# When additions of weights are issued in attention, and which of two ready pieces of work goes first at the start of the MLP

## The chip, the core and the metric

The kernel runs on one core of a Trainium2 chip. The metric is the time of one execution in device microseconds (us). Five engines work side by side, each through its own list of instructions in a fixed order: TensorE (PE) multiplies and transposes, VectorE (DVE) and ScalarE (ACT) do elementwise work, GpSimd (POOL) does some elementwise work and issues the DMAs that add to HBM, and SyncE (SP) issues the other DMAs. An engine whose next instruction waits runs nothing that stands behind it.

## The reference

One decoder layer on x of 512 tokens by 1024 channels, in float32:

```python
h = rms_norm(x, norm_mix)
u, q, kc, vc, ksl, vsl, kwn, vwn, g_nsa, g_merge = split(h @ w_in)
y_pool = pool_mixer(u, w_pool, pool_scale)
y_nsa  = nsa_mixer(q, kc, vc, ksl, vsl, kwn, vwn, g_nsa, ...)   # 16 heads
g_a, g_b = split(sigmoid(g_merge))
x = x + (g_a * (y_pool @ w_proj_pool) + g_b * (y_nsa @ w_proj_nsa)) @ w_out
h = rms_norm(x, norm_mlp)
x = x + square(relu(h @ w_ff1)) @ w_ff2
return rms_norm(x, norm_final)
```

The attention has a compressed, a selected and a window branch. With 512 tokens, all eight blocks of keys are selected.

## The kernel before

**Precision.** A float32 operand of a large product is split into a high part (a copy in a reduced form, by ACT) and a low part (the rest, by DVE). A product is the sum of high times high, high times low and low times high.

**Strassen-like products.** The gates, `w_out` and the MLP use seven products of quarters where eight would be plain: `A11, S3, S1, S2, A12, A22, S4`. The names beginning with S need sums of quarters of the weights. The kernel makes these sums in HBM: a *job* is first a copy of one quarter into a scratch tensor, issued by SP (`make_sum`, line 340), and then an accumulating DMA that adds the other quarter to it, issued by POOL (`add_sum`, line 348). There are 55 jobs, numbered 0 to 54 in the order of their copies. Copied jobs whose addition has not been emitted stand in the queue `begun`, the oldest first.

**Loads.** All weights pass through 170 loads of 512 KB or less, numbered 0 to 169, into six buffers named `raw`. `emit_load` (line 299) issues the next load and behind it the copies that are due at it (`sums_after`). A load leaves the table `raws` when both of its parts have been converted. Loads 37 to 49 are the weights of the gate and of the queries that fill up PE in attention (`FILL2`), 50 to 57 those of `w_proj_nsa`, 58 to 71 those of `w_out`, 72 and later those of the MLP. By `sums_after`, job 16 is copied behind load 47, jobs 17 and 18 behind 48, 19 behind 49, 20 and 21 behind 50, and one each (22 to 25) behind loads 51 to 54. Jobs 17, 20 and 25 copy a sum that is itself a job (9, 12 and 21), so `make_sum` first emits all additions up to that job. From load 54 on, `emit_load` emits one addition at each load while more than two jobs are in `begun`.

**Attention.** Scores are worked off in 96 slots, twelve for each of eight pairs of heads. In slot i PE forms the scores of i+1 and turns the probabilities of slot i-4 (line 1440), DVE masks and takes the maximum of i (line 1400), ACT takes the exponential (line 1410), and POOL multiplies the probabilities of slot i-1 by the reciprocal of their sum and by the gate (`weight`, line 1423). Every third slot after the seventh, when no rotation of queries is under way (`scored["rope"]`), an addition may be emitted behind that multiplication (`add_sum(last)`). Such an addition is tied to its slot by `tc.issue_after`; additions that `make_sum` and `emit_load` emit have no such tie.

**Order.** The kernel is written as one sequence with generators that interleave; a planner then fixes each engine's order ahead of time. It takes what it expects to be ready, by priority, which is the place in the program unless `high_priority` raises it. `behind(ins)` puts what follows on the engine of `ins` after it in that order, without a wait of its own.

**The start of the MLP.** `Mixed` multiplies the merged mixers by `w_out`. Its `take` adds the products to x (line 1706 for `S1` and `A22`), sums the squares, scales the tokens (`scaled`: a reciprocal, line 1602, and two multiplications, line 1612) and turns them on PE in `to_fm` (line 1864). Tokens come in four tiles of 128: tiles 0 and 1 after `A22`, tiles 2 and 3 after `S4` (line 565). `S4` accumulates in the two PSUM tiles of `S1`, so it waits until line 1706 has read them. The scaled tiles go through the turning into high and low parts (line 1868 and 1871). Then come the MLP's first products on PE (line 635), for two groups 0 and 1, called in the order `A11100, A11101, A12100, A12101`: the product's name, the layer, the chunk, the group. `A12100` accumulates on `A11100`'s PSUM tile, after ACT has copied that tile (line 650). All PSUM tiles here carry one tag with eight buffers, and the program asks for them in the order: `A11100`, two for turning token tile 2, `A11101`, two for tile 3.

Of the kernel before, what the change touches and what calls it, by code (L numbers as in the profile page):

```python
# [62 lines left out]
def trunk(ctx: ExitStack, tc: tile.TileContext, A, out):  # L63
    nc = tc.nc
    PE, ACT, DVE, POOL = nc.tensor, nc.scalar, nc.vector, nc.gpsimd
# [104 lines left out]
    for k in P1 + FILL2:  # L170
        if k[-2] == "G":
            g, o = int(k[-1]), k[:-2]
# [15 lines left out]
    late, later, wo_of = [], [], []  # L188
# [80 lines left out]
    raws, hls = {}, {}  # L269
    st = {"load": 0, "prep": 0, "use": 0, "kept": 0, "pairs": 0, "sums": 0, "spared": 0}  # L270
    spare, slots_hl = [], []
    held, begun = {}, deque()

    began, conv = [None], [None]

# [57 lines left out]
    def make_sum(load):  # L333

        if st["sums"] < len(jobs):
            to, q, _ = jobs[st["sums"]]
            while any(q is jobs[n][0] for n in begun):
                add_sum()
            with tc.issue_after(load.ins):
                nc.sync.dma_start(to, q)  # L340
            begun.append(st["sums"])
            st["sums"] += 1

    def add_sum(behind=None):

        to, _, q = jobs[begun.popleft()]
        with tc.issue_after(behind.ins) if behind else nullcontext():
            POOL.dma_start(to, q, accum_op=ALU.add)  # L348

    part, first_of, held_back, roots, summed = {}, [], [], [], []  # L350
# [231 lines left out]
    def step_side():  # L582
        for _ in range(len(side)):
            g = side.popleft()
            try:
                next(g)
                side.append(g)
            except StopIteration:
                pass
# [9 lines left out]
    def product(ps, key, first, mm):  # L599

        w, n = use(key), 0
        for f in range(2):
            for low in range(2):
                for k, u, v in [(k, low, v) for k in range(4) for v in range(2 - low)]:
                    mm(ps[:, 256 * f:256 * f + 256], w, f, k, u, v, start=first and n == 0, stop=n == 23,
                       skip_group_check=True)
                    n += 1
                    if n % 6 == 0:
                        step_side()
                        ahead()  # L610

    def until(ready):
        while not ready():
            assert side
            step_side()

    class Group:


# [6 lines left out]
        def pe(self, o):  # L626
            until(lambda: o not in self.NEEDS or self.NEEDS[o] in self.done)
            if not self.done:
                side.append(self.main())
            name, x, *at = self.X[o]  # L630
            until(lambda: self.of(x))
            moving = self.of(x)

            def mm(out, w, f, k, u, v, **kw):
                PE.matmul(out, w[u][:, k, 128 * f:128 * f + 128], moving[v][:, k, :], **kw)  # L635
            if not at:
                self.ps[name] = self.bank()
            product(self.ps[name], o + self.key, not at, mm)
            if at:
                side.append(self.last(name, *at))  # L640
            self.done.add(o)
# [30 lines left out]

    hT = (R1, R2)
    f_banks = [2]
    last_mm = [None]

    def fm_products(wH, wL, xT, sub=0, nk=8, tok=slice(0, S)):
        prods = []
# [104 lines left out]
    def behind(made):  # L783
        return tc.issue_after(made.ins)
# [41 lines left out]
    r, _ = evac0(1)  # L826
    with behind(r):
        r, scaled2 = sums0(2)
# [4 lines left out]
    with behind(conv[0]):  # L833
        root3, v = sums0(3)
# [34 lines left out]
    scored = {"pairs": 0, "rope": 0}  # L869
# [70 lines left out]
    with ExitStack() as c1:  # L940
# [254 lines left out]
        for k in P1[2:]:  # L1195
            i = int(k[-1]) if k[-1].isdigit() else None
            if k[-2] == "G":
                if not gate_f:
                    t = p1.tile([128, 16, 128], FR, tag="cA", bufs=1, name="gs")
# [29 lines left out]
            elif k[:2] == "pp":  # L1229
                w = use(k)  # L1230
# [17 lines left out]
    with ExitStack() as c2:  # L1248
# [200 lines left out]
        def turn_hi(i):  # L1449
            src, dH, dL = turn_views(i)  # L1450
            his.append(ACT.activation(dH, src, AF.Copy))  # L1451
# [46 lines left out]
        for i in range(n + LAG + PLAG):  # L1498
            if i < n:
                p = slots[i][0]  # L1500
                if i % 12 == 3 and p + 1 < NPAIR:
                    while p + 1 not in Q:
                        fill()
                        step_side()
                if i % 12 == CMP_AT and p + 1 < NPAIR:
                    side.append(cmp_scores(p + 1))
            if i + 1 < n:
                score_pe(i + 1)
                scored["pairs"] = (i + 2) // 12
            t = i - LAG  # L1510
            if 0 <= t < n:
                turn_pe(t)
                turn_hi(t)
            if i < n:
                smax(i)
                expo(i)
            if 0 <= i - 1 < n:
                last = weight(i - 1)
                slot.update(long=i > 3 and slots[i - 1][1] == 1, scaled=last)
            if i > 7 and i % 3 == 0 and not scored["rope"] and len(begun) > 2:  # L1520
                add_sum(last)
            if 0 <= t < n:
                slot["low"] = turn_lo(t)
            step_side()
            want = done0 + (total - done0) * (i + 1) // (n + LAG + PLAG)
            while fdone[0] < want and fill():
                pass
            if i < 5:
                fill()
            if turning:  # L1530
                turn_c()
            j = t - PLAG
            if 0 <= j < n and j % 2 == 1 and pv(j):
                o_evac(*slots[j][0:2])
# [185 lines left out]
    with ExitStack() as c3:  # L1720
# [7 lines left out]
        for m, keys in enumerate(("A112o0 A122o1 S42o0", "A112o1 A222o0 S42o1", "S32o0 A222o1 A11100", "S32o1 S12o0 A11101")):  # L1728
            for k in keys.split():
                o = 1024 * m + 8 * (k[:2] in ("S1", "S3", "A2"))  # L1730
# [70 lines left out]
        class Mixed(Wide):  # L1801
# [25 lines left out]
            def take(self, o, ps):  # L1827
                yield from super().take(o, ps)
                if o == "S2":
                    for i, j in ((1, 0), (1, 1), (0, 1)):  # L1830
                        for f in range(2):
                            x = XX[:, 2 * j + f, 512 * i:512 * i + 512]
                            DVE.tensor_tensor(x, x, self.U[:, f, :], op=ALU.subtract if i else ALU.add)
                            yield
                elif o == "A12":
                    for t in range(2):
                        square_sum(t, 0)
                elif o == "S1":
                    for t in range(2, 4):
                        square_sum(t, 1, 0)  # L1840
                elif o == "A22":
                    for t in range(2):
                        square_sum(t, 1)
                    xs = [scaled(t) for t in range(2)]
                    while "S1" not in self.done:
                        yield
                    for t in range(2):
                        yield from to_fm(t, xs[t])

        def scaled(t):  # L1850
            xs = q3.tile([128, D], F32, tag="xs", bufs=2, name="xs")
            normed(t, xs)
            return xs

        def to_fm(t, xs=None):
            if xs is None:
                xs = scaled(t)
                for _ in range(3):
                    yield
            th, sl = t // 2, slice(128 * (t % 2), 128 * (t % 2) + 128)  # L1860
            for a in range(2):
                pt = bank()
                for k in range(4):
                    PE.transpose(pt[:, 128 * k:128 * k + 128], xs[:, 512 * a + 128 * k:512 * a + 128 * k + 128], ident)
                src = pt[:, :].rearrange("p (k c) -> p k c", k=4)
                b = f"{a + 1}{th + 1}"
                if b != "12":
                    ACT.activation(XB[b][0][:, :, sl], src, AF.Copy)
                ACT.activation(XQ[b][:, :, sl], src, AF.Copy)
                if b != "12":  # L1870
                    DVE.tensor_tensor(XB[b][1][:, :, sl], src, XB[b][0][:, :, sl].bitcast(F32), op=ALU.subtract)
                yield
            shaped.append(t)
            if th == 0:
                return
            for o, d, x, y in (("T1", XT, XQ["11"], XQ["12"]), ("T3", XQ["12"], XQ["22"], XQ["12"]),
                               ("T2", XQ["11"], XQ["22"], XT)):
                DVE.tensor_tensor(d[:, :, sl], x[:, :, sl], y[:, :, sl], op=ALU.add if o == "T2" else ALU.subtract)
                while o not in XB:
                    yield  # L1880
                ACT.activation(XB[o][0][:, :, sl], d[:, :, sl], AF.Copy)
                yield
                DVE.tensor_tensor(XB[o][1][:, :, sl], d[:, :, sl], XB[o][0][:, :, sl].bitcast(F32), op=ALU.subtract)
            turned[0] += t == 3
# [206 lines left out]
    t, o = 3, out_of(3)  # L2091
# [3 lines left out]
    with tc.high_priority(64):  # L2095
        ACT.activation(junk[0], ps, AF.Square, accum_out=sq[:, t, 1:2])
        r = rms(t)
# [22 lines left out]
```

## Time and profile before

| | |
|---|---|
| median of three runs | 766.87 us (766.41 to 767.01) |
| the profiled execution | 766.66 us |
| its span, first to last instruction | 764.9 us |
| around the span | 1.8 us |
| mean granted TensorE clock | 0.997 of 2.4 GHz |
| stretch of the attention's slots | about 172 to 362 us |
| start of the MLP | about 437 to 453 us |

Times inside the profile count from the start of the span. In a timeline row stand the start, the busy time, the engine, the line, the operation, the shapes and how many instructions were merged; in brackets the idle time of that engine just before, and what ended it by the profile.

### The profile page before, as it was taken

The page shows a single profiled execution, that of the slowest core. Times are in us where ns is not written, and L with a number is a line of the kernel's source. Part 1 is how long each engine was busy: PE and PEld are TensorE (multiplying, and loading weights), DVE is VectorE, ACT ScalarE, POOL GpSimd, SP SyncE. Part 2 cuts the span into 40 slices and gives each one's busy share as a digit, 9 for nine tenths or more (in the row PEclk, how much of TensorE's full clock was granted, in tenths as well). Part 3 has the DMA queues.
Part 4 walks back from the last instruction along what each step waited for, and adds up shares of the span by engine and source line. Part 5 has one row for each costly group of instructions (what it writes and reads, how often), then busy time and mean ns, then how long its engine had stood idle before and what let it go on. Part 6 is the DMA issues. An engine that isn't in the chain of part 4 may idle for free.

```text
span 764.9 us, 13254 instructions
## 1 busy us (share of the span) xinstructions
PE 752.9 (98%) x4661; PEld 669.7 (88%) x4661; DVE 670.8 (88%) x1282; ACT 513.2 (67%) x977; POOL 190.5 (25%) x269
## 2 busy tenths in 40 slices
PE   8999999999999999999999999999999999999996
PEld 7889999888888888888888799989998999899985
DVE  7998989549989889989689999998899788978897
ACT  7777655328878888898746576944774477447754
POOL 5001010117747876875000020111111111110001
PEclk9999999999999999999999999999999999999998
DMA  9869886986063945675383699979999999798532
GB/s 303 227 177 275 230 245 143 250 215 165 18 204 83 224 94 115 121 139 111 89 296 133 218 272 249 298 210 325 290 269 211 315 307 263 206 313 252 195 109 110
DMA packets 120285, 158.09 MB, mean 207 GB/s; under 512 B 6006, under 2 KB 88474, under 8 KB 119963
## 3 DMA queue, kind: packets, MB, share of 16 engines
q1 hardware_dynamic: 98058, 127.62, 51.2%
q0 software_dynamic: 21872, 28.84, 24.4%
q10 hardware_dynamic: 288, 0.79, 0.3%
q8 instruction: 37, 0.61, 0.3%
q14 instruction: 30, 0.24, 0.1%
HBM read 152.50 MB, written 59.77 MB: 278 GB/s over the span
## 4 chain that ended last, share of the span: by engine, by line
PE 87%; DVE 6%; ACT 2%; DMA 2%; issue 1%; POOL 1%; ACTq 0%; DVEq 0%; POOLq 0%; SPq 0%
PE psB L1685 21%; PE psB L635 21%; PE psF L565 18%; PE psV L635 5%; PE psB L565 4%; PE psS L1378 4%; PE psO L1474 3%; PE psT L1440 3%; PE psV L565 2%; PE psF L697 2%; DMA S<-w_ff 1%; PE psC L997 1%; DVE P L1400 1%; DVE PT L1456 1%; PE psT L565 1%
## 5 line engine op out<-in xcount | busy, mean ns | idle before, releaser
L348 POOL DMA_DIRECT2D S<-w_ff x44 | 49.3, 1124 | 334.1 <-DMA S<-w_ff 247.9
L395 ACT ACTIVATE wh<-raw 128x1024 fp32r<-128x1024 f32 x72 | 76.1, 1058 | 75.6 <-PE psB L635 28.3
L565 PE MATMUL psF<-R,wh 128*128 128x512 f32 x384 | 124.5, 400 | 0.0
L1423 POOL TENSOR_SCALAR P<-P,sm,GT 128x128 f32<-128x128 f32 (+3 forms) x128 | 91.0, 798 | 45.5 <-DVE sm L1420 25.4
L401 DVE TENSOR_TENSOR wl<-raw,wh 128x1024 fp32r<-128x1024 f32 x72 | 87.9, 1221 | 10.2 <-ACT wh L395 9.7
L565 PEld LDWEIGHTS psF<-R,wh 128*128 128x128 f32 x384 | 68.8, 188 | 11.2
L1410 ACT ACTIVATE P<-P,sm 128x128 f32<-128x128 f32 (+3 forms) x128 | 71.0, 557 | 9.6 <-DVE sm L1400 6.3
L565 PE MATMUL psF<-R,wl 128*128 128x512 f32 x192 | 75.5, 393 | 0.0
L521 ACT ACTIVATE wh<-raw 128x512 fp32r<-128x512 f32 (+1 forms) x76 | 45.1, 616 | 31.0 <-PE psF L565 21.2
L1400 DVE CUSTOM_DVE_ANT_0 P<-psS,cst 128x128 f32<-128x128 f32 (+3 forms) x128 | 59.5, 483 | 5.2 <-PE psT L1440 3.7
L395 ACT ACTIVATE w3h<-raw 128x1024 fp32r<-128x1024 f32 x36 | 38.1, 1058 | 36.9 <-PE psB L635 15.4
L524 DVE TENSOR_TENSOR wl<-raw,wh 128x512 fp32r<-128x512 f32 (+1 forms) x74 | 50.9, 697 | 11.0 <-ACT wh L521 10.2
L1451 ACT ACTIVATE PT<-psT 128x512 fp32r<-128x512 f32 (+2 forms) x96 | 49.0, 520 | 13.8 <-PE psT L1440 12.8
L1456 DVE TENSOR_TENSOR PT<-psT,PT 128x512 fp32r<-128x512 f32 (+2 forms) x96 | 56.2, 592 | 1.2 <-ACT PT L1451 1.0
L1440 PE MATMUL psT<-ident,P 128*128 128x128 f32 x320 | 50.2, 273 | 0.3 <-POOL P L1423 0.3
L401 DVE TENSOR_TENSOR w3l<-raw,w3h 128x1024 fp32r<-128x1024 f32 x36 | 44.0, 1222 | 5.6 <-ACT w3h L395 5.4
L1474 PE MATMUL psO<-PT,VV 128*128 128x256 f32 x320 | 48.5, 286 | 0.0
L635 PE MATMUL psB<-R,wh 128*128 128x256 f32 x336 | 46.7, 279 | 0.7 <-ACT GB L650 0.7
L1440 PEld LDWEIGHTS psT<-ident,P 128*128 128x128 f32 x320 | 39.5, 140 | 8.8 <-POOL P L1423 0.8
L635 PEld LDWEIGHTS psB<-R,wh 128*128 128x128 f32 x336 | 42.6, 188 | 1.1 <-ACT GB L650 0.9
L1474 PEld LDWEIGHTS psO<-PT,VV 128*128 128x128 f32 x320 | 42.2, 188 | 1.3 <-ACT PT L1451 0.3
L565 PEld LDWEIGHTS psF<-R,wl 128*128 128x128 f32 x192 | 36.0, 188 | 7.5
(450 smaller groups left out, 2074.6 us busy)
## 6 DMA issues: line engine op xcount, KB each, us to landing
raw<-w_ff SPq DMA_DIRECT2D x54, 512.0 KB, 6.0
S<-w_ff POOLq DMA_DIRECT2D x44, 512.0 KB, 8.5
raw<-S SPq DMA_DIRECT2D x44, 512.0 KB, 5.6
S<-w_ff SPq DMA_DIRECT2D x32, 512.0 KB, 7.6
raw<-w_in SPq DMA_DIRECT2D x31, 512.0 KB, 5.4
S<-S SPq DMA_DIRECT2D x12, 512.0 KB, 5.8
S_o<-w_out POOLq DMA_DIRECT2D x8, 512.0 KB, 7.8
raw<-w_proj_nsa SPq DMA_DIRECT2D x8, 512.0 KB, 4.5
```

The lines of the kernel that those rows point to most:

```text
L395: ACT.activation(h, t, AF.Copy)
L401: DVE.tensor_tensor(l, t, h.bitcast(F32), op=ALU.subtract)
L524: eng.tensor_tensor(l[:, sl], t[:, sl], h[:, sl].bitcast(F32), op=ALU.subtract)
L565: PE.matmul(ps, a, b, start=first and j == 0, stop=last and j == n - 1, skip_group_check=True)
L635: PE.matmul(out, w[u][:, k, 128 * f:128 * f + 128], moving[v][:, k, :], **kw)
L1400: DVE.tensor_tensor_reduce(out=P[:, o:o + n].rearrange("p (a c) -> p a c", c=128), in0=s, in1=m, scale=1.0, scalar=3e38, op0=ALU.add, op1= ...
L1410: last_exp[:] = [ACT.activation(c, c, AF.Exp, bias=sm[:, 0, e:e + 1], scale=-1.0, accum_out=sm[:, 1, e:e + 1])]
L1423: r = POOL.tensor_scalar(P[:, o:o + n], P[:, o:o + n], sm[:, 2, e:e + 1], GT[:, qb, c + e:c + e + 1], op0=ALU.mult, op1=ALU.mult)
L1440: PE.transpose(pt[:, 128 * j:128 * j + 128], P[:, 128 * j:128 * j + 128], ident)
L1456: return DVE.tensor_tensor(dL, src, dH.bitcast(F32), op=ALU.subtract)
L1474: PE.matmul(ps[:, qb % 2, :, :], VV[:, k, b, g, :], t[:, j, :, :], start=False, stop=last and j == len(kbs) - 1 and t is tL, skip_group_ch ...
L1685: PE.matmul(ps[f], self.Y.of(y)[u][:, 2 * g + k, 128 * f:128 * f + 128], w[v][:, k, :], start=first and g == k == u == v == 0, stop=g == k ...
```

## The change

Three edits. In the attention, an addition is emitted when at least two jobs are in `begun` and every load up to the second one after the oldest job's copy has been converted, where before it was emitted when more than two jobs were in `begun`. The first multiplication of `A12100` is put behind the last of the latest `A11` product, which is `A11101`'s. Token tile 1's scaling is emitted after `S1` has been taken and put behind `S1`'s additions to x on DVE.

```diff
+    held, begun, born = {}, deque(), {}
...
             begun.append(st["sums"])
+            born[st["sums"]] = st["load"] - 1
             st["sums"] += 1
+
+    def landed():
+
+        return len(begun) > 1 and min(raws, default=st["load"]) > born[begun[0]] + 2
...
-            if i > 7 and i % 3 == 0 and not scored["rope"] and len(begun) > 2:
+            if i > 7 and i % 3 == 0 and not scored["rope"] and landed():
                 add_sum(last)
...
             def mm(out, w, f, k, u, v, **kw):
-                PE.matmul(out, w[u][:, k, 128 * f:128 * f + 128], moving[v][:, k, :], **kw)
+                late = o + self.key == "A12100" and f == k == u == v == 0
+                with behind(last_mm[0]) if late else nullcontext():
+                    r = PE.matmul(out, w[u][:, k, 128 * f:128 * f + 128], moving[v][:, k, :], **kw)
+                if o == "A11":
+                    last_mm[0] = r
...
-                    xs = [scaled(t) for t in range(2)]
+                    xs = scaled(0)
                     while "S1" not in self.done:
                         yield
-                    for t in range(2):
-                        yield from to_fm(t, xs[t])
+                    with behind(summed[0]):
+                        other = scaled(1)
+                    yield from to_fm(0, xs)
+                    yield from to_fm(1, other)
```

(`last_mm = [None]` moves up to stand before the class that now uses it.)

## Rows read from the trace of the kernel before

**Rows 1.** The page: busy time and share of each engine.

```profile
PE 752.9 (98%) x4661; PEld 669.7 (88%) x4661; DVE 670.8 (88%) x1282; ACT 513.2 (67%) x977; POOL 190.5 (25%) x269
```

**Rows 2.** Busy time by stretch: length, PE, PEld, DVE, ACT, POOL, clock, DMA.

```profile
172.00:362.00 190.00, 188.35 (x1220) 165.75 (x1219) 172.64 (x578) 161.96 (x443) 130.45 (x193) 1.00 0.58 126
...
438.00:453.00 15.00, 13.70 (x93) 12.20 (x92) 14.46 (x25) 11.06 (x26) 5.36 (x5) 1.00 1.04 305
453.00:742.00 289.00, 289.00 (x1908) 265.28 (x1907) 261.21 (x312) 182.11 (x243) 26.42 (x24) 1.00 0.92 257
```

**Rows 3.** What PE waited for, attention's slots, then 380 us to the end.

```profile
PE psS L1378 <- DVE sm L1400: 1.1, 3, 0.5
PE psT L1440 <- POOL P L1423: 0.3, 1, 0.3
PE psO L1465 <- ACT PT L1451: 0.3, 1, 0.3
...
PE psB L635 <- ACT GB L650: 0.7, 1, 0.7
PE psB L565 <- DVE x L1706: 0.6, 1, 0.6
```

**Rows 4.** The chain of waits between 255 and 280 us: start, us, what.

```profile
260.24 10.00 DMA S<-w_ff
```

**Rows 5.** Timeline of POOL in attention.

```profile
230.65 1.10 POOL L348 DMA_DIRECT2D S<-w_ff  x1 [1.21 <-DMA S<-w_ff]
...
244.96 1.07 POOL L348 DMA_DIRECT2D S_o<-w_out  x1
...
253.23 2.06 POOL L348 DMA_DIRECT2D S_o<-w_out  x1
256.53 1.17 POOL L348 DMA_DIRECT2D S<-w_ff  x1 [1.24 <-DVE sm L1420]
...
270.87 1.19 POOL L348 DMA_DIRECT2D S<-w_ff  x1 [4.98 <-DVE PT L1456]
```

**Rows 6.** Timeline of SP in attention: issues of copies.

```profile
220.01 0.59 SPq L340 DMA_DIRECT2D S<-w_ff  x1
...
224.93 0.59 SPq L340 DMA_DIRECT2D S<-w_ff  x1
...
244.91 0.54 SPq L340 DMA_DIRECT2D S<-S  x1
...
275.16 0.59 SPq L340 DMA_DIRECT2D S<-w_ff  x1
```

**Rows 7.** Attention's additions (line 348): from issue to landing.

```profile
DMA to landing us min/median/max: 6.1/6.4/11.5
```

**Rows 8.** Timeline of PE at the start of the MLP.

```profile
437.04 1.14 PE L1864 MATMUL psB<-ident,xs 128*128 128x128 f32 x9
438.80 0.47 PE L565 MATMUL psB<-W1H,mH 128*128 128x512 f32 x1 [0.61 <-DVE x L1706]
...
445.19 1.10 PE L635 MATMUL psB<-R,W1H 128*128 128x256 f32 x8
...
448.86 0.51 PE L635 MATMUL psB<-R,wh 128*128 128x256 f32 x2 [0.69 <-ACT GB L650]
...
449.88 0.60 PE L1864 MATMUL psB<-ident,xs 128*128 128x128 f32 x4
450.23 0.95 PE L635 MATMUL psB<-R,W1H 128*128 128x256 f32 x6
```

**Rows 9.** Timeline of DVE in the same stretch.

```profile
435.12 1.42 DVE L1612 SCALAR_TENSOR_TENSOR xs<-x,sq,gB 128x512 f32<-128x512 f32 x2
...
437.97 1.28 DVE L1706 TENSOR_TENSOR x<-x,psB 128x512 f32<-128x512 f32 x2
439.17 1.22 DVE L401 TENSOR_TENSOR W1L<-raw,W1H 128x1024 fp32r<-128x1024 f32 x1
...
447.61 1.41 DVE L1612 SCALAR_TENSOR_TENSOR xs<-x,sq,gB 128x512 f32<-128x512 f32 x2
```

More of the change, by code (lines that the diff above doesn't have):

```diff
@@ L271, in trunk @@
     spare, slots_hl = [], []
-    held, begun = {}, deque()
+    held, begun, born = {}, deque(), {}
     began, conv = [None], [None]
@@ L615, in until @@
             step_side()
+    last_mm = [None]
     class Group:
@@ L674, in trunk @@
     f_banks = [2]
-    last_mm = [None]
     def fm_products(wH, wL, xT, sub=0, nk=8, tok=slice(0, S)):
```

## The prediction

> **What bounds the kernel now.** I read the page first. PE is busy 98% of the span [rows 1], so only two things can shorten the kernel: less work on PE, or less idle time of PE. The change removes no multiplication and no transposition, so all of its gain or loss must be PE's idle time. Busy time by stretch shows where that idle time is [rows 2]. From 453 to 742 us there is none: 289.00 us busy of 289.00. In attention's slots PE lacks 1.65 us of 190, and at the start of the MLP 1.30 us of 15. Both are places that the change touches. What PE waited for names the pieces [rows 3]: in attention three waits on DVE's maxima (1.1 us in all), one on ACT (0.3) and one on POOL (0.3); at the start of the MLP one on ACT's copy of `A11100`'s tile (0.7) and one on `S1`'s additions by DVE (0.6). These sum to 3.0 us. That is the ceiling of what the change can win.
>
> After 453 us PE never waits, so what PE gains or loses before then reaches the end, unless a later stage has it waiting for something else. DMA's share there is 0.92 [rows 2], so there is little room for transfers that are pushed into it.
>
> The chain of waits shows what the attention's edit is about [rows 4]: a copy for a sum, issued at 260.24, took 10.00 us, and POOL's addition stood waiting for it. The timeline of POOL says the same, with a name that misleads [rows 5]: the addition at 270.87 was preceded by 4.98 us of idle time, put down to a DVE instruction; but the copy landed at 260.24 + 10.00 = 270.24, and the addition followed 0.63 us behind. The multiplications of the probabilities stood behind it, and PE lost 0.3 us to them [rows 3].
>
> **Which additions the new test moves.** I followed the two conditions through the program's own counters, slot by slot. Before, of the 17 additions emitted in the slots (jobs 7 to 23), ten are tied to a slot (7, 10, 11, 13 to 18, 23), and seven (8, 9, 12, 19 to 22) are emitted without a tie, because a copy needs an earlier sum or because load 54 is reached. The timeline shows what a missing tie does [rows 5]: jobs come in order of number in the program, yet job 19's addition, at 230.65, stands ahead of job 7's, at 244.96, the first of the two into `w_out`. The planner puts an untied addition where it expects the copy to have landed: 19's copy was issued at 224.93 [rows 6].
>
> With the new test, jobs 7 and 10 stay in slots 36 and 39. Job 11 (the one at 253.23) fails in slot 42, since load 45 is not converted, and is then emitted untied when load 50 needs job 12. Job 13 goes from slot 60 to 75, and 14, 15 and 16 move on by three slots each, to 78, 81 and 84. Jobs 17, 18 and 23 lose their ties: 17 and 18 are emitted when load 54 needs job 21, job 23 when load 55 is reached. Job 22, the one that stalled POOL at 270.87, is untied before and after. So the edit does not make that addition wait for its copy in the program; it changes the company the copy travels in. Nothing is issued later than the last tied addition of before, and copies and loads keep their order.
>
> **The price in attention, part by part.** *Job 11 leaves 253.23.* It probably goes ahead of the slots, before 172 us, where POOL has nothing to multiply. Between 244.96 and 270.24, 25.3 us, five additions (the first at 244.96, the last at 256.53) and three copies for sums (the first at 244.91 [rows 6], the last at 260.24) ran beside a few loads: at most an estimated 25.3 / 8 = 3.2 us each. One fewer lands job 22's copy up to 3.2 us earlier, and POOL's 4.98 us wait falls to as little as 1.8. Since the whole wait cost PE 0.3 us [rows 3], the bounds are 0 and -0.3. I take -0.3: what is left of the stall is likely to be covered by the slots that lie between POOL's multiplication and PE's turning.
>
> *Jobs 17 and 18 come early.* Their copies are issued one behind the other, the second at 220.01 [rows 6]. Uncrowded, a copy lands in about 5.1 us (job 19's: 230.65 less the 0.63 us between landing and issue, less 224.93). So these additions are probably issued at about 225 and 226, while job 19's copy, issued at 224.93, is under way. At 3.2 us each they delay it by up to 6.4 us, and job 19's wait of 1.21 us grows to as much as 7.6. The nearest row for such a wait is the 4.98 us one, which cost 0.3 us; beyond that I count one for one. Bounds: 0 and 0.3 + 2.6 = +2.9. I take +0.1: the three overlap only in part, and a wait near 4 us is below the row's.
>
> Here the profile and a page differ. An addition alone took at least 6.1 us from issue to landing, at the median 6.4 [rows 7]. The Trainium skill, DMA: Bandwidth & Descriptors, section Anatomy of one DMA, gives a fit of 2.0 us plus the bytes over 436 GB/s, 3.2 us for 512 KB. By it POOL would hardly wait for either copy, and both terms would be nothing.
>
> *Job 23 is untied.* Its copy, at 275.16 [rows 6], has no addition beside it but job 22's. The addition comes at about 281 instead of at the attention's end; a wait of up to 2 us lies inside what the 4.98 us wait shows to be nearly free. 0. *Jobs 13 to 16* have landed long before; each addition takes POOL about 1.1 us wherever it stands [rows 5], and POOL is busy for 130 of 190 us [rows 2]. 0. Should the cover go, each costs its 1.1 us.
>
> **The price at the start of the MLP.** *Token tile 1's scaling.* DVE scales tile 0 at 435.12 for 1.42 us, then tile 1, and only at 437.97 takes `S1` [rows 9]. PE had issued `S1` by 437.04 and waits 0.61 us for that until 438.80 [rows 8]. After the change `S1` is taken at about 436.8 and `S4` can begin at about 438.0, when the eight transpositions of tile 0 are through. This saves PE 0.6 to 0.8 us at that point. But DVE runs on without a pause afterwards, 14.46 of 15 us [rows 2], and the same instructions remain. A gap of about 0.25 us arises between 436.54 and 436.8, as nothing else may go there: the low parts of the next weights are themselves behind `S1`. So tile 2's scaling, at 447.61 [rows 9], comes about 0.25 us later.
>
> *`A12100` behind `A11101`.* `A11101` has the same tokens as `A11100`, which starts at 445.19, and its weights' low part is made from 439.17 on [rows 9]. Yet `A12100` went first, at 448.86 with 0.69 us of waiting, and `A11101` followed only at 450.23, right behind the turning of token tile 2 [rows 8]. The one thing left that can hold it is its PSUM tile, which the program asks for after the two of tile 2. I take it that tiles of a tag are given out in the program's order. Then PE has nothing to run between `A11100` and tile 2's turning after the change: the wait on ACT goes, and a wait on tile 2 takes its place. Scaling of tile 2 ends at 449.02 + 0.25; its last four transpositions follow at 449.33 and end, at the 0.35 us of before, at 449.68. The four multiplications of `A12100` that ran before this point, and now do not, cost half of the 1.10 us that eight take at 445.19, 0.55 us. Equal work is done at 450.23, as before. I take 0 for both edits together. Bounds: -1.3 if both waits go for good, and +1.2 if one of DVE's conversions of 1.22 us [rows 9] comes ahead of a scaling.
>
> **Sum.** -0.3 + 0.1 + 0 = -0.2 us on the profiled execution: 766.66 - 0.2 = 766.46, a span of 764.7 and 1.8 around it. The median of the runs is 0.21 above that execution, so I write 766.6.
>
> **The rivals.** *Both waits at the MLP's start go.* If the tile order does not hold `A11101`, PE runs from `A11100` through it, the 0.69 is covered, and `S4`'s 0.6 stays won, as the first `S1100` product has data in time. 766.87 - 1.3 - 0.2 = 765.4, and down to 764.4 as the planner's new order also removes up to 1.0 us of attention's other 1.4; its middle is 764.9. For it: both waits are plainly there [rows 3]. Against it: the place of `A11101`, and DVE's full stretch.
>
> *A new stall in attention takes the old one's place.* Job 19's copy shares the DMA engines with two additions and POOL stands still for over 5 us at about 230, where its multiplications run back to back. From a wait of 5 us on, PE loses one for one; at the bound of 7.6 us that is 766.87 - 0.3 + 2.9 = 769.5, and at 6.3 us 768.2. For it: 10.00 us for a crowded copy [rows 4]. Against it: there are two additions in company there and not five. The Trainium skill, SBUF — State Buffer, section "Can I just issue two DMAs to hit both halves?", states that concurrent DMAs serialize on the same 16 engines; the 10.00 us agree with that.
>
> *DVE decides at the MLP's start.* A conversion gets ahead of tile 1 or 2's scaling: 766.87 - 0.2 + 1.2 = 767.9.
>
> *Nothing moves.* The tie to slots hardly mattered and the MLP's waits only change names: 766.9.
>
> **How the numbers follow.** A measurement of this kernel can tell about 0.2%, 1.5 us, from no change. The forecast (766.6, give or take 0.9) has 0.45 and nothing-moves 0.08; the MLP's waits going 0.26; the new stall 0.13; DVE 0.08. Faster by over 0.2% means under 765.3, half of all of PE's idle time: 0.22, of it 0.20 from the first rival and the rest from the forecast's tail. Slower means over 768.4: 0.17, from the new stall, half of DVE's and some unforeseen order. Same: 0.61. The range from 764.9 to 768.4 leaves out about one in ten at either end.
>
> **What would show it right or wrong.** In the changed kernel's trace: POOL's additions at about 225 and 226, and none at 253; the wait ahead of job 22's addition cut to half; a longer one at job 19's. On PE, `S4` at about 438.0 without a wait on line 1706; `A11101` right behind tile 2's turning and ahead of `A12100`, with PE idle for about 1 us between `A11100` and that turning. If `A11101` follows `A11100` at once, the tile order was a wrong reading, and the time is below 765.8. If PE waits on POOL by more than 1 us in attention, the second rival holds. PE's busy time within 453 to 742 without a gap is a condition of all this; a wait on a conversion there would break it.

## The result, and the profile of the changed kernel

The changed kernel takes 770.73 us (median of 7 runs, 770.18 to 774.33); the kernel before took 766.87 beside it (7 runs, 766.41 to 768.94). The ratio is 1.0055, 95% interval 1.0044 to 1.0066: slower by about 4 us, where 766.6 was forecast. The profiled execution took 770.95 us with a span of 769.2, 4.3 more than before.

The page's line of busy times answers to [rows 1]; the work is the same, instruction for instruction.

```profile
PE 754.1 (98%) x4661; PEld 669.6 (87%) x4661; DVE 673.1 (88%) x1282; ACT 513.5 (67%) x977; POOL 190.7 (25%) x269
```

Busy time by stretch, with the columns of [rows 2] and the stretches moved by what the changed kernel is late:

```profile
172.00:366.00 194.00, 188.95 (x1219) 165.49 (x1218) 175.04 (x577) 162.38 (x443) 130.59 (x193) 1.00 0.55 121
...
442.00:457.00 15.00, 13.68 (x93) 12.08 (x93) 14.88 (x26) 11.04 (x26) 5.34 (x5) 1.00 1.04 306
457.00:746.00 289.00, 289.00 (x1909) 265.32 (x1908) 260.81 (x312) 181.68 (x243) 26.43 (x24) 1.00 0.92 257
```

PE lacks 194.00 - 188.95 = 5.05 us in attention, against 1.65 before. At the start of the MLP it lacks 1.32 against 1.30, and behind it nothing, as before. So the loss lies in attention, 3.40 us of it in idle time. What PE waited for (us in total, times, longest) answers to [rows 3]:

```profile
PE psT L1450 <- POOL P L1433: 2.1, 3, 1.6
PE psB L1876 <- DVE xs L1622: 1.2, 1, 1.2
...
PE psS L1388 <- DVE sm L1410: 0.8, 2, 0.5
PE psT L1358 <- DVE PT L1466: 0.8, 1, 0.8
PE psT L1358 <- POOL PC L1345: 0.7, 1, 0.7
...
PE psT L1450 <- POOL rx L909: 0.4, 1, 0.4
```

POOL was waited for by 0.3 us before; now it is 2.1 + 0.7 + 0.4 = 3.2. The timeline of PE says where:

```profile
173.30 0.54 PE L1358 MATMUL psT<-identR,PC 128*128 128x128 f32 x4 [0.68 <-POOL PC L1345]
...
240.51 0.66 PE L1450 MATMUL psT<-ident,P 128*128 128x128 f32 x4 [1.55 <-POOL P L1433]
...
284.34 0.65 PE L1450 MATMUL psT<-ident,P 128*128 128x128 f32 x4 [0.24 <-POOL P L1433]
...
285.78 0.65 PE L1450 MATMUL psT<-ident,P 128*128 128x128 f32 x4 [0.32 <-POOL P L1433]
...
294.56 0.51 PE L1358 MATMUL psT<-identR,PC 128*128 128x128 f32 x4 [0.78 <-DVE PT L1466]
...
311.37 0.63 PE L1450 MATMUL psT<-ident,P 128*128 128x128 f32 x4 [0.37 <-POOL rx L909]
```

Waits at five places (284 and 286 are one), none of which stands in the trace of before. That one has waits of 0.2 to 0.3 us at 239, 244 and 275 in their stead, for ACT, DVE and POOL. The timeline of POOL answers to [rows 5]; the additions are line 353 now:

```profile
225.38 1.20 POOL L353 DMA_DIRECT2D S<-w_ff  x1 [2.64 <-DMA S<-S]
226.97 1.04 POOL L353 DMA_DIRECT2D S<-w_ff  x1 [0.40 <-issue]
227.57 2.20 POOL L1433 TENSOR_SCALAR P<-P,sm,GT 128x256 f32<-128x256 f32 x3
229.40 1.06 POOL L909 TENSOR_TENSOR rx<-rx,cst 128x256 f32<-128x256 f32 x1
233.11 1.07 POOL L353 DMA_DIRECT2D S<-w_ff  x1 [2.65 <-DMA S<-w_ff]
...
268.98 1.20 POOL L353 DMA_DIRECT2D S<-w_ff  x1 [1.34 <-DMA S<-w_ff]
...
282.28 1.19 POOL L353 DMA_DIRECT2D S<-w_ff  x1 [0.81 <-DVE sm L1410]
```

The additions of jobs 17, 18 and 23 stand where the prediction put them: at 225.38, 226.97 and 282.28. Job 19's, at 230.65 before, is issued at 233.11. Its copy, SP's second line below, left 0.26 us behind the first of the two additions and landed 6.93 us later; before it took 5.08.

```profile
225.22 0.37 SPq L299 DMA_DIRECT2D raw<-w_in  x1
225.64 0.59 SPq L340 DMA_DIRECT2D S<-w_ff  x1
```

At the MLP's start PE and DVE answer to [rows 8] and [rows 9]:

```profile
441.79 0.47 PE L570 MATMUL psB<-W1H,mH 128*128 128x512 f32 x1
...
448.72 1.09 PE L644 MATMUL psB<-R,W1H 128*128 128x256 f32 x8
...
452.93 1.38 PE L1876 MATMUL psB<-ident,xs 128*128 128x128 f32 x8 [1.22 <-DVE xs L1622]
454.06 0.95 PE L644 MATMUL psB<-R,W1H 128*128 128x256 f32 x6
...
439.13 1.42 DVE L1622 SCALAR_TENSOR_TENSOR xs<-x,sq,gB 128x512 f32<-128x512 f32 x2
440.95 1.28 DVE L1716 TENSOR_TENSOR x<-x,psB 128x512 f32<-128x512 f32 x2 [0.41 <-PE psB L1695]
...
452.12 1.41 DVE L1622 SCALAR_TENSOR_TENSOR xs<-x,sq,gB 128x512 f32<-128x512 f32 x2
```

Token tile 0's turning starts 4.17 us later than before (441.21 against 437.04 [rows 8]): that is attention's whole loss, the 3.40 us of idle time and 0.60 of longer busy time (188.95 against 188.35 [rows 2]) included. `S4` now starts without a wait, and `A11100` is only 3.53 us late (448.72 - 445.19). Then PE waits 1.22 us for tile 2's scaling, which DVE begins only at 452.12. `A11101` follows, ahead of `A12100`. The two edits give 0.64 us and take it back.

### The profile page after: what moved, and what is told of

It is laid out like the page before. It is cut to its first block, busy times and chain, and to the rows that moved or that the text cites. A ratio compares the mean times of both kernels' runs of the same rounds, so it can differ in the third digit from the quotient of the medians.

```text
span 769.2 us, 13258 instructions
## 1 busy us (share of the span) xinstructions
PE 754.1 (98%) x4661; PEld 669.6 (87%) x4661; DVE 673.1 (88%) x1282; ACT 513.5 (67%) x977; POOL 190.7 (25%) x269
## 4 chain that ended last, share of the span: by engine, by line
PE 56%; DVE 4%; issue 1%; ACT 1%; POOL 0%; POOLq 0%; DVEq 0%; ACTq 0%
PE psB L1695 22%; PE psB L644 20%; PE psF L570 4%; PE psB L570 4%; PE psO L1484 2%; PE psT L1450 2%; PE psS L1388 1%; PE psT L570 1%; DVE x L2057 0%; DVE MA L1622 0%; DVE x L1716 0%; DVE R L1883 0%; DVE wl L406 0%; DVE R L406 0%; DVE P L1410 0%
```

## The experiments

Theory A: additions without a tie stand ahead of POOL's multiplications where POOL has no slack, and PE waits for these. The rivals: B, the MLP's edits cost it; C, the DMA engines are fuller, whatever POOL's order; D, jobs 13 to 16, moved to later slots, cost it. Each run's ratio is to runs of the kernel before on the same chip, with its 95% interval; it is not the quotient of the two medians. The profile is of one execution; a second profile of the changed kernel differs from the first by 0.9 us of PE's waiting around 240 alone, so places go by the profiles, and sizes by the ratios and by several profiles together.

**The attention's edit alone.** The MLP's two edits are undone.

```
-                late = o + self.key == "A12100" and f == k == u == v == 0
+                late = False
-                    xs = scaled(0)
+                    xs = [scaled(t) for t in range(2)]
...
```

> The attention's edit alone: both edits at the start of the MLP are undone. Theory A (untied additions ahead of POOL's multiplications): all of the loss stays, PE is idle for about 5.0 us in attention as in the changed kernel (1.65 before), and the time is 770.2 to 770.8. Theory B (the edits at the MLP's start cost it, through what the planner makes of them elsewhere): 766.5 to 767.5.

Measured: 1.0035 (1.0020 to 1.0050), 770.42 us. B falls. Its profile, of the fastest of its eleven runs (768.60 us), shows the waits at 284, 294 and 311 (here 0.32, 0.77 and 0.41 us), but hardly any of the one at 240: POOL waited only 0.65 us ahead of job 19's addition. So PE was idle for 3.31 us in attention (172 to 366), and not for the 5.0 expected.

**The MLP's two edits alone.**

```
-            if i > 7 and i % 3 == 0 and not scored["rope"] and landed():
+            if i > 7 and i % 3 == 0 and not scored["rope"] and len(begun) > 2:
```

> The two edits at the start of the MLP alone: additions in attention under the old condition. Theory A: attention is as before (1.65 us of idle PE), the waits at the MLP's start only change names, 766.7 to 767.3. Theory B: 769.5 to 771.

Measured: 0.9999 (0.9984 to 1.0014), 767.31 us, 1.72 us of idle PE in 172 to 362 and 1.32 in 438 to 453, with the same 1.22 us ahead of tile 2's turning. These edits are worth nothing that shows.

**Ties given back.** In `add_sum`, an addition emitted without a tie gets one, to the multiplication of the slot in which it stood before:

```
...
+        if begun[0] in TIED and not behind:
+            behind = slot[TIED[begun[0]]]
         to, _, q = jobs[begun.popleft()]
...
```

`TIED` is {17: 84, 18: 87} in the first kernel, with 11: 42 and 23: 90 as well in the second, and {23: 90} in the third.

> The changed kernel, but the additions of jobs 17 and 18 are tied to the slots in which they stood before (84 and 87). Theory A: no addition at 225 and 227, job 19's is issued at about 231, PE's wait of 1.6 us for POOL at 240 goes, and the losses at 173, 282 and 294 stay: about 1.2 to 1.9 us of the loss come back, 768.9 to 769.6. Theory C (the loss comes from how full the DMA engines are, whatever POOL's order is): POOL's additions only move elsewhere, less than 0.5 us comes back, 770.3 to 770.8.

> The changed kernel, but all four additions that lost their ties or their place (jobs 11, 17, 18 and 23) are tied to the slots of before; what is left of the attention's edit is that jobs 13 to 16 are added three to fifteen slots later. Theory A: PE's idle time in attention falls back to 1.65 us, give or take 0.5, and the time is 766.6 to 767.5. Theory D (the later jobs 13 to 16 are to blame): 769.5 or more.

> The changed kernel, but job 23's addition is tied to slot 90 again. Theory A: the waits of PE at 284, 286 (POOL's multiplications, 0.9 us in all in the changed kernel) and the 0.94 us at 294 behind them go, as with all four ties; the rest stays: 1.2 to 1.9 us below the changed kernel. Theory E (the 0.94 us at 294 belong to DVE's own order): only 0.5 to 0.9 us come back.

Measured: 17 and 18 tied 1.0035 (1.0023 to 1.0047), 769.85 us, a little above theory A's range; all four 1.0015 (1.0001 to 1.0029), 768.23 us, between the ranges of A and D; 23 alone 1.0018 (1.0000 to 1.0035), 767.82 us, where the changed kernel beside it had 1.0046. With 17 and 18 tied, job 19's addition waits 1.30 us and POOL costs PE nothing around 240. With 23 tied, the waits at 284 and 286 go and DVE's at 294 with them, in both kernels: that wait too is a consequence of job 23's addition. With all four tied, one wait of 0.38 us for POOL's `rx` at 309 stays in attention that the kernel before does not have; it is in every profile with jobs 13 to 16 in their later slots and in none with the old condition (one of these, that of the run on `A11101`'s tile below, has 0.32 us for DVE there). So D holds a part, within the 0.01 to 0.29% by which this kernel is still slower.

**The changed kernel once more.**

> The changed kernel once more, unaltered, beside the next kernels on one chip. If the single profile is typical: PE waits for POOL by over 1 us at about 240 and by about 0.5 at 285, and the time is 0.4 to 0.7% above that of before. If job 19's crowded copy varies from execution to execution (in the attention's edit alone job 19's addition waited 0.65 us and not 2.65), the wait at 240 is below 0.5 us in some profiles and the loss is 0.3 to 0.55%.

Measured: 1.0046 (1.0029 to 1.0062), 769.74 us. The profiled execution was a long one (773.26 us, span 771.5). POOL's additions in its timeline, and the two waits of PE for `P` around 240 in that of the kernel with job 23 tied, whose profile shows the same stall:

```profile
225.00 1.20 POOL L353 DMA_DIRECT2D S<-w_ff  x1 [2.60 <-DMA S<-S]
227.78 1.04 POOL L353 DMA_DIRECT2D S<-w_ff  x1 [1.59 <-DVE sm L1410]
...
235.15 1.07 POOL L353 DMA_DIRECT2D S<-w_ff  x1 [3.90 <-DVE sm L1430]
```

```profile
236.96 0.55 PE L1454 MATMUL psT<-ident,P 128*128 128x128 f32 x3 [2.48 <-POOL P L1437]
242.52 0.66 PE L1454 MATMUL psT<-ident,P 128*128 128x128 f32 x4 [1.55 <-POOL P L1437]
```

The name behind 3.90 misleads, as in [rows 5]: job 19's copy, issued at 225.31, took 9.30 us and landed at 234.61, 0.54 ahead of the addition. In the kernel with 23 tied it took 9.34. PE waited 2.44 us for it in the one and 4.03 in the other. In the first the wait cost more than itself, by the stretches ahead of it and behind it (columns of [rows 2]):

```profile
230.00:234.00 4.00, 4.00 (x29) 3.67 (x28) 3.44 (x10) 2.56 (x7) 1.25 (x2) 1.00 1.11 235
238.00:242.00 4.00, 4.00 (x18) 3.39 (x18) 2.57 (x8) 2.48 (x6) 3.75 (x7) 0.63 0.62 112
```

TensorE's granted clock, 1.00 up to 236, was 0.50 of 2.4 GHz, the lower of its two levels, from 238 to 240, and a multiplication of 512 columns took 0.63 us instead of 0.40. PE's instructions were 3.0 us later than in the kernel before when it went on (236.99 against 233.98) and 4.6 us later at 241.26 (against 236.63). In the kernel with 23 tied the clock stayed at 1.00 behind a wait of 2.48 us. Why it fell in the one and not in the other stays open.

**The two additions at an eighth of their size.** Seven eighths of these two sums are left out.

```
...
+        if n in (17, 18):
+            to, q = to[0:16], q[0:16]
```

> The changed kernel, but the additions of jobs 17 and 18 add only the first 16 of 128 rows (an eighth of the bytes; the rest of these two sums is left out). They stand where they stood in POOL's order. If the price of these two is the crowding of job 19's copy, that copy takes about 5.1 us instead of 6.9, job 19's addition is issued at about 231.4 instead of 233.1, and PE's wait at 240 falls below 0.5 us: 1.2 to 1.7 us below the changed kernel. If it is POOL's place and time (two additions of about 1.1 us ahead of the multiplications), over 1 us of PE's waiting for POOL between 234 and 241 stays, and less than 0.6 us comes back.

Measured: 1.0024 (1.0009 to 1.0038), against 1.0046 beside it: 1.7 us come back by the ratios, but only 0.5 by the medians (769.28 against 769.74), and the intervals overlap. Job 19's copy takes 5.75 us, its addition is issued at 231.50, and PE's wait for `P` around 240 is 0.76 us. The copy's time speaks for the crowding, as the prediction had it, and it is back among the times of unaccompanied copies (4.8 to 5.8 us); the two additions also take POOL 0.83 and 0.80 us instead of 1.20 and 1.04, which the run does not tell apart. The 0.76 us is over the bound named for that (0.5), as POOL waited 1.78 us ahead of the addition, 0.57 longer than before; yet such a wait needs no addition beside the copy, as the next run shows. A and C look like one mechanism here: a crowded copy, and multiplications that stand behind its addition.

**`A11101`'s PSUM tile first.** Old condition in attention; both tiles are asked for ahead of the first product.

```
...
+            for g in gs0 if o == "A11" else ():
+                g.ps["a"] = bank()
             for g in gs0:
```

> The two edits at the MLP's start alone (old condition in attention), and both PSUM tiles of A11100 and A11101 asked for ahead of the first product. If the order of the PSUM tiles holds A11101 back, as the prediction took it: A11101 follows A11100 at once, PE's 1.2 us of waiting for tile 2's scaling goes, and the time is 1.0 to 1.3 us below that of the two edits alone, 765.6 to 766.2. If something else holds it: nothing changes, 766.7 to 767.3.

Measured: 1.0004 (0.9990 to 1.0018), and the same 1.22 us ahead of tile 2. The order in which tiles are asked for is not what holds `A11101`. In attention, under the old condition, job 19's copy took 5.81 us with no addition beside it; POOL waited 1.96 us ahead of the addition, and PE 0.98 us for POOL at 239.

**Tile 2 turned behind `A11101`.** Old condition in attention.

```
...
-                for _ in range(3):
+                while not begun_both:
                     yield
...
-                g.pe(o)
+                g.pe(o), begun_both.extend([g] * (g is gs0[1]))
```

> The two edits at the MLP's start alone, and token tile 2 is turned only after A11101 has been emitted, so that both its PSUM tiles and its transpositions come behind A11101 in the program. PE's 1.2 us of waiting for tile 2's scaling is then covered by 24 multiplications of A11101: 0.9 to 1.3 us below the two edits alone, 766.0 to 766.4. Rival: a later product then waits for tile 2 or 3 by as much, 767.0 to 767.5.

Measured: 0.9991 (0.9983 to 1.0000), 766.26 us against 766.87. PE runs through `A11101` and six multiplications of `A12100` into the turning without a wait; a later product then waits 0.61 us for DVE:

```profile
449.39 1.10 PE L644 MATMUL psB<-R,W1H 128*128 128x256 f32 x8
450.33 0.64 PE L644 MATMUL psB<-R,W1L 128*128 128x256 f32 x4
450.81 0.87 PE L644 MATMUL psB<-R,wh 128*128 128x256 f32 x6
451.51 1.03 PE L1876 MATMUL psB<-ident,xs 128*128 128x128 f32 x8
...
475.75 0.36 PE L644 MATMUL psB<-xT4H,wh 128*128 128x256 f32 x1 [0.61 <-DVE MA L668]
```

The place in the program decided: with the turning emitted later, the planner puts `A11101` first. Half of the 1.22 us is given back later, and the interval reaches to 1: the best kernel of the study, but not shown to be faster.

**Job 19 tied as well.** With the old condition and the MLP's edits, alone and together with the foregoing; and in the changed kernel with 17, 18 and 23 tied, there through `TIED`, which then has 19: 36 too.

```
-        to, _, q = jobs[begun.popleft()]
+        behind, (to, _, q) = behind or (slot[36] if begun[0] == 19 else None), jobs[begun.popleft()]
...
```

> The two edits at the MLP's start alone (old condition in attention), and job 19's addition tied to slot 36, some 15 us later, so that POOL does not stand waiting for its copy at 230. Theory A: what PE loses at 237 to 242 with this addition in place (0.4 us in the kernel before, 0.85 and 1.14 in the profiles of the two kernels with its attention) goes or nearly so: 0.3 to 0.9 us below the two edits alone, 766.2 to 766.8, and no POOL wait over 0.3 us there. Rival: the multiplications there are late for another reason (DVE's maxima), nothing changes, 767.0 to 767.5.

> Both of the foregoing: job 19's addition tied to slot 36 and token tile 2 turned behind A11101. If the two gains add up: 765.2 to 766.0, a ratio of 0.997 to 0.9985 to the kernel before. If one of them is given back later: within 0.4 us of the better of the two alone.

> The changed kernel with the additions of jobs 17, 18 and 23 in the slots of before and job 19's in slot 36; jobs 11 and 13 to 16 stay where the attention's edit put them. Theory A: of the loss only the 0.5 to 0.7 us at 309 to 311 stays, and what PE lost around 240 goes too: 766.6 to 767.6. Rival (moving jobs 11 and 13 to 16 is a price of its own, of over 1 us): 768 or more.

Measured: 1.0015 (1.0000 to 1.0030), 1.0007 (0.9995 to 1.0019) and 1.0017 (1.0006 to 1.0028). The gains hoped for in the first two did not come (768.66 and 767.65 us); the third, 767.42, lies in theory A's range. Around 240 the wait for POOL goes, as theory A says, but the stall moves. Job 19's addition now travels with the five behind 244, and the copies beside them get slower: job 22's took 13.27 us in the first kernel against 10.00 [rows 4]. In the first kernel POOL stands waiting ahead of the additions at 258 and 273, and PE behind it:

```profile
258.56 1.18 POOL L353 DMA_DIRECT2D S<-w_ff  x1 [3.83 <-DVE sm L1430]
273.20 1.19 POOL L353 DMA_DIRECT2D S<-w_ff  x1 [6.10 <-DVE wl L529]
```

```profile
260.61 0.66 PE L1450 MATMUL psT<-ident,P 128*128 128x128 f32 x4 [0.81 <-POOL P L1433]
...
274.93 0.74 PE L1450 MATMUL psT<-ident,P 128*128 128x128 f32 x2 [0.89 <-POOL P L1433]
```

In the third kernel, in which job 11 is out of that company, job 22's copy took 9.52 us, POOL waited 4.17 and 3.07 us ahead of the same two additions, and PE did not wait behind them: 1.62 us of idle PE in attention, as in the kernel before (1.65). This is the good that the attention's edit did. The kernel is still slower in the ratio (1.0006 at least); the profile is of its fastest run.

```profile
172.00:362.00 190.00, 188.38 (x1219) 165.56 (x1219) 172.69 (x578) 162.34 (x443) 128.16 (x192) 1.00 0.56 123
```

## Why the prediction was wrong

*The step that failed* is the price of POOL's delays. The prediction took it from one row at 270, where 4.98 us of POOL's waiting cost PE 0.3, and so put jobs 17 and 18 at +0.1 us and job 23 at 0. The runs showed POOL's multiplications with little or no slack at 230 and at 280 to 290. What each place costs can be read from the traces without naming a wait: take how much later an instruction of PE starts than the same one in the kernel before, and see by how much that grows over a stretch (times of the kernel before, us).

| stretch | what was moved there | changed kernel | other profiles with that move | profiles without it |
|---|---|---|---|---|
| 226 to 246 | 17 and 18 early | +1.1 | +0.2, +3.5, +3.6 | -0.2 to +0.2 (five); small additions -0.05 |
| 281 to 296 | 23 early | +1.9 | +1.6 to +1.9 (four) | 0.0 (eight) |
| 306 to 330 | 13 to 16 late | +0.8 | +0.8 to +1.0 (seven) | 0.0 to +0.5 (five) |

The first row leaves out the three kernels in which job 19's addition is moved too. With 0.65 us at 173 and small terms the three make up the 4.3 us of the changed kernel's profile.

*Bound.* Right: PE's work is the same, and the loss is for the most part PE's idle time, all of it ahead of 453 us.

*Which additions move, and where to.* Right in every one, the three places included.

*Job 22's wait.* Its size was right, its worth was not. The copy landed in 6.44 us instead of 10.00 and POOL's wait fell from 4.98 to 1.34 us, below the 1.8 forecast. PE's 0.3 us at 275 became a wait of 0.16 for DVE at 277. Little was to be won there. The two edits of the MLP alone also came to 0.15 us for DVE at that place, with job 11 where it was.

*Jobs 17 and 18: a term that was too small.* Taken at +0.1 with bounds 0 and +2.9. The ratios give 1.7 us (1.0046 against 1.0024), 1.5 against the tied kernel on another chip (1.0055 less 1.0035), and nothing where that kernel and the attention's edit alone stood on one chip (1.0035 both). The profiles have 0.2, 1.1, 3.5 and 3.6 us: the price varies from execution to execution, and its mean is not settled. The two large ones stand in long executions (773.26 us beside a median of 769.74, and 771.19 beside 767.82). The mechanism agrees with the one named, job 19's crowded copy. The price per wait was wrong: it was read from [rows 5]'s 4.98 us, which cost PE 0.3, and that row is from 270. At 230 POOL's multiplications run back to back. Its slack can be read from one run to the next: behind waits of 1.21 [rows 5] and 1.30 us (17 and 18 tied) ahead of job 19's addition PE did not wait for POOL, though 0.5 us in all for ACT and DVE; behind 1.78 it waited 0.76 us (the small additions), behind 1.96 us 0.98 (`A11101`'s tile first, old condition), behind 2.65 us 1.55, behind 3.90 us 2.44, and behind 5.11 us 4.03 (23 tied). Here PE begins to wait beyond 1.3 us, and every wait is 1.0 to 1.5 us less than POOL's, where the prediction let one for one begin at 5. At 270 the old row holds: 6.10 us of waiting cost 0.89.

*Job 23: taken as 0 without bounds.* Measured at about 2.1 us by the ratios (1.0046 against 1.0018; 1.5 with job 11 tied as well, 1.0035 against 1.0015), and at 1.6 to 1.9 us in every profile that has the move: the best shown of the terms. Each difference of two ratios is uncertain by some 1.7 us (two intervals of 0.15 to 0.17% either way), so which of the two terms is larger on average is not shown. The addition waited 0.81 us only, so the argument about a wait was beside the point. POOL's multiplications from 280 to 290 run back to back as well, and one addition of 1.19 us among them makes PE wait twice (0.24 and 0.32) and pushes DVE's work, for which PE waits 0.78. The sentence "each addition takes POOL about 1.1 us wherever it stands, and POOL is busy for 130 of 190 us" is an average that does not hold there.

*Jobs 13 to 16.* Taken as 0. The wait for `rx` at 311, 0.37 us, is theirs by the kernel with four ties, and PE falls 0.8 to 1.0 us behind between 306 and 330 in every profile that has them late. By which mechanism is not shown.

*The wait at 173.* 0.68 us in the first profile, yet it is not the change's: over the profiles it is from 0 to 0.29 in the six others with job 11 early, and 0 to 0.94 in seven with job 11 at its old place or under the old condition. What makes it vary stays open.

*The MLP's start.* Its sum was right: 0 taken, 0.64 won and 0.77 lost measured (`S4`, then tile 2), a ratio of 0.9999 alone. `A11101` came where it was said. The reason given for that, the order of PSUM tiles, fell: asking for the tile first changed nothing, and emitting the turning later did.

*The rivals.* "A new stall in attention takes the old one's place", with 0.13, is what happened, and "PE waits on POOL by more than 1 us" the sign of it. It was priced at 768.2 to 769.5, below the 770.73 measured, and only at one of its places.

Not tried: how job 23 or 19 would fare tied to other slots, and a version with job 11 early and all else as before.

## What to carry to other kernels

How long an in-order engine may stand waiting is a property of the place: look at the stretch behind the wait, and whether the engine's instructions run back to back there, before taking a price from a wait elsewhere. An average busy share says nothing on that. Compare the starts of the same instruction in both traces: a list of waits leaves out what a wait does to the work behind it. And an operation that loses its tie is not "free": it is put where its data are expected, ahead of whatever is there, and tying the next one can merely move the crowd, as job 19's did.

## What the runs showed of the hardware

Job 19's copy took 4.8 to 5.8 us where no addition was issued beside it, and 5.44 where it left 0.58 us ahead of the first one (the attention's edit alone). Where it left at the first one's time or up to 0.31 us behind it, with the second 1.3 to 2.5 us behind the copy, it took 6.93, 9.34 and 9.30; with these two cut to an eighth of their bytes, 5.75. In both of the 9.3 us cases SP's own instruction for the copy took 1.2 to 1.4 us instead of 0.59; but so it did in the run with small additions and in that on `A11101`'s tile, whose copies took 5.75 and 5.81. The Trainium skill, SBUF — State Buffer, section "Can I just issue two DMAs to hit both halves?", states that concurrent DMAs serialize on the same 16 engines, as measured there on tiles in SBUF; here the transfers go from HBM to HBM, and the 6.93 to 9.34 us against 5.75 with fewer bytes agree. Unexpected was the spread of one and the same program: 6.93 and 9.30 us for the same copy, and 1.55 and 2.44 us of PE's waiting.
